# A layer norm with GELU: ten of 64 tiles take their statistics on ScalarE, and beta's split moves

**Chip, cores, metric.** One core of one Trainium2 chip. The metric is the device time of one execution in microseconds (us). Medians and ratios are of fast runs alone, and every profiled run was a fast one, with a granted clock of 1.0. "Span" is the time from the first to the last instruction in a profiled execution; it is some 1.8 us shorter than the device time.

## What is computed

```python
# x: (8, 1024, 2048) float32, gamma, beta: (2048,), eps = 1e-5
mean = np.mean(x, axis=-1, keepdims=True)
var = np.var(x, axis=-1, keepdims=True)
out = gamma * (x - mean) / np.sqrt(var + eps) + beta
return 0.5 * out * (1 + np.tanh(np.sqrt(2 / np.pi) * (out + 0.044715 * out ** 3)))
```

The 8192 rows are 64 tiles of 128 rows by 2048 columns, 1 MB each.

## The kernel before

```python
groups = [2, 2] + [4] * 14 + [2, 1, 1]        # tiles whose 1/sqrt is taken together

def reciprocal_sqrt(nc, pool, ve, n):          # all on GpSimd, on 128 x n
    nc.gpsimd.tensor_scalar(out=y..., in0=ve..., ...)           # first guess from the bits (L23)
    for _ in range(3):                                          # Newton
        nc.gpsimd.tensor_tensor(out=t, in0=y, in1=y, op=MUL)    # L26
        nc.gpsimd.tensor_tensor(out=t, in0=t, in1=ve, op=MUL)   # L27
        nc.gpsimd.tensor_scalar(out=t, in0=t, scalar1=-0.5, scalar2=1.5, op0=MUL, op1=ADD)  # L28
        nc.gpsimd.tensor_tensor(out=y, in0=y, in1=t, op=MUL)    # L29
    return y

def stats(i):                                  # VectorE, then GpSimd once a group
    # [cut: st, mv]
    for c in range(nbank):
        nc.vector.bn_stats(out=st[:, c, :], in_=xts[i][:, c * BANK:(c + 1) * BANK])  # L111
    nc.vector.bn_aggr(out=mvs[g][:, k, :], in_=st)                                   # L112
    if k == size - 1:
        # ve = var + eps (L115); y = reciprocal_sqrt(...); nmr = -(mean * y) (L118, L119)

def normalize(j):                              # ScalarE: y * x + nmr, in place (L125)
def affine(j):                                 # VectorE: ps[j % 2] = xt * gamma (L130),
                                               # TensorE adds beta from b_rows (L133)
def gelu(j):                                   # ScalarE: ps -> xt (L137), store, load tile j + 16

# step s: stats(s); normalize(j); affine(j - 1); gelu(j - 2).
# In the middle j = s - 5: a group's first tile is normalized two steps after
# the statistics of its last.
```

The two tiles `ps` in PSUM, the memory in which TensorE adds beta, matter: a multiplication (`affine(j)`) must wait for `gelu(j - 2)`, which reads the same one. Every engine takes its instructions in program order. [Cut: pools, loads of the first 20 tiles, the launch.]

## Time and profile before

| | before |
|---|---|
| device time, median | 342.36 us |
| span | 340.6 us |
| VectorE busy | 310.5 us (91%) |
| ScalarE busy | 247.6 us (73%) |
| GpSimd busy | 132.3 us (39%) |
| moved by DMA | 135.4 MB, 398 GB/s mean |

In the groups of the profile a row is: line, engine, operation, output and input, count; busy us and mean ns of one; idle time of the engine just ahead of these, and what ended it. In a timeline a row is: start, us, engine, line, operation, count; in brackets the engine's wait ahead of it.

### The profile page before, as it was taken

Reading aid. Unit: us, or ns where it says so; the run is one execution under the profiler, and the core shown is the slowest. Engines: PE = TensorE matmul, PEld = TensorE weight load, DVE = VectorE, ACT = ScalarE, POOL = GpSimd, SP = SyncE. Lnnn points to the kernel's source line nnn. Section 1 sums busy time; section 2 is a strip of 40 time slices with the busy share of each in tenths; the row PEclk is TensorE's granted clock in tenths of the full one; section 3 lists DMA queues with packets and bytes.
Section 4 is the critical chain, followed back from the end, with each engine's and each line's share of the span. In section 5 each row is a group of like instructions: output and inputs, shape, how many; then the busy total and the mean of one; then the engine's idle time right before and its main releaser. Section 6 shows DMA issues by size and latency. Waiting matters only on the chain.

```text
span 340.6 us, 1787 instructions
## 1 busy us (share of the span) xinstructions
PE 122.6 (36%) x264; PEld 35.0 (10%) x264; DVE 310.5 (91%) x391; ACT 247.6 (73%) x130; POOL 132.3 (39%) x308
## 2 busy tenths in 40 slices
PE   4003242343234324432443244324432443245521
PEld 1000010111011101110111011101110111011100
DVE  3799999999999999999999999999999999996640
ACT  0149297886959598786959688695969868698962
POOL 0350307043250806234170714325080523788820
DMA  7999999999999999999999999999999999865556
GB/s 298 416 420 418 420 420 422 428 425 423 425 427 426 426 423 425 425 427 424 427 427 426 425 426 425 427 426 423 426 427 424 426 425 424 352 255 246 247 216 277
DMA packets 19164, 135.41 MB, mean 398 GB/s; under 512 B 2640, under 2 KB 2640, under 8 KB 2640
## 3 DMA queue, kind: packets, MB, share of 16 engines
q1 hardware_dynamic: 18576, 135.27, 94.9%
q10 hardware_dynamic: 576, 0.02, 0.1%
q14 instruction: 10, 0.08, 0.1%
q8 instruction: 2, 0.03, 0.0%
HBM read 68.17 MB, written 67.11 MB: 397 GB/s over the span
## 4 chain that ended last, share of the span: by engine, by line
issue 45%; POOL 36%; DVE 10%; DMA 5%; ACT 1%; PE 1%; POOLq 0%; SPq 0%; ACTq 0%
POOL t L26 12%; POOL ve L115 9%; DVE st L111 6%; POOL t L28 5%; DMA xt<-in_x_dram 4%; DVE ps L130 4%; POOL y L29 4%; POOL t L27 3%; POOL nmr L118 2%; DMA bt<-in_beta_dram 1%; ACT xt L137 1%; POOL nmr L119 1%; POOL y L23 1%; PE ps L133 1%; DVE mv L112 0%
## 5 line engine op out<-in xcount | busy, mean ns | idle before, releaser
L133 PE MATMUL ps<-b_rows,ones 3*128 3x512 bf16 x256 | 119.0, 616 | 209.8 <-DVE ps L130 209.8
L125 ACT ACTIVATE xt<-xt,nmr,y 128x2048 f32<-128x2048 f32 x64 | 133.4, 2086 | 54.8 <-POOL nmr L119 54.8
L111 DVE BATCH_NORM_STATS2 st<-xt 128x6 f32<-128x512 f32 x256 | 157.2, 676 | 2.3 <-DMA xt<-in_x_dram 2.2
L130 DVE TENSOR_TENSOR ps<-xt,g_t 128x2048 f32<-128x2048 f32 x64 | 145.6, 2276 | 10.3 <-ACT xt L137 10.3
L137 ACT ACTIVATE xt<-ps 128x2048 f32<-128x2048 f32 x64 | 119.4, 1868 | 24.0 <-PE ps L133 23.9
L115 POOL TENSOR_SCALAR ve<-mv 128x4 f32<-128x4 f32 (+2 forms) x19 | 31.7, 1666 | 169.6 <-DVE mv L112 169.4
L133 PEld LDWEIGHTS <-ones 3*128 3x128 bf16 x256 | 34.0, 133 | 294.8 <-issue 294.8
L26 POOL TENSOR_TENSOR t<-y 128x4 f32<-128x4 f32 (+2 forms) x57 | 44.6, 782 | 4.6
L112 DVE BATCH_NORM_AGGREGATE mv<-st 128x2 f32<-128x24 f32 x64 | 16.9, 264 | 3.2
L28 POOL TENSOR_SCALAR t<-t 128x4 f32<-128x4 f32 (+2 forms) x57 | 17.3, 303 | 5.0
L29 POOL TENSOR_TENSOR y<-y,t 128x4 f32<-128x4 f32 (+2 forms) x57 | 13.3, 233 | 4.8
L27 POOL TENSOR_TENSOR t<-t,ve 128x4 f32<-128x4 f32 (+2 forms) x57 | 11.4, 199 | 4.5
L125 ACT ACT_TABLE_LOAD x1 | 1.3, 1283 | 9.3 <-DVE st L111 9.3
L118 POOL TENSOR_TENSOR nmr<-mv,y 128x4 f32<-128x4 f32 (+2 forms) x19 | 5.9, 310 | 1.5
L119 POOL TENSOR_SCALAR nmr<-nmr 128x4 f32<-128x4 f32 (+2 forms) x19 | 4.3, 229 | 1.7
L82 DVE CAST part<-bt 128x16 bf16<-128x16 f32 x3 | 0.5, 174 | 4.7 <-DMA bt<-in_beta_dram 4.6
L23 POOL TENSOR_SCALAR y<-ve 128x4 int32<-128x4 int32 (+2 forms) x19 | 3.7, 194 | 1.6
L91 PE MATMUL ps<-zeros 1*128 1x512 bf16 x8 | 3.6, 626 | 1.3 <-DVE zeros L78 1.3
L91 PEld LDWEIGHTS <-zeros 1*128 1x128 bf16 x8 | 1.0, 137 | 3.0 <-issue 1.7
L137 ACT ACT_TABLE_LOAD x1 | 1.3, 1283 | 0.0
L76 DVE MEMSET ones<- 3x128 bf16 x1 | 0.2, 165 | 0.8 <-PEq L191 0.8
L84 DVE TENSOR_TENSOR bt<-bt,part 128x16 f32<-128x16 f32 x2 | 0.3, 175 | 0.1
(5 smaller groups left out, 0.7 us busy)
## 6 DMA issues: line engine op xcount, KB each, us to landing
xt<-in_x_dram SPq DMA_DIRECT2D x64, 1024.0 KB, 19.1
out_dram<-xt SPq DMA_DIRECT2D x64, 1024.0 KB, 17.0
g_t<-in_gamma_dram SPq DMA_DIRECT2D x1, 1024.0 KB, 11.5
b_rows<-part ACTq DMA_DIRECT2D x3, 4.0 KB, 9.9
bt<-in_beta_dram ACTq DMA_DIRECT2D x1, 8.0 KB, 5.1
```

The costliest lines, as they stand in the source:

```text
L26: nc.gpsimd.tensor_tensor(out=t, in0=y, in1=y, op=MUL)
L27: nc.gpsimd.tensor_tensor(out=t, in0=t, in1=ve, op=MUL)
L28: nc.gpsimd.tensor_scalar(out=t, in0=t, scalar1=-0.5, scalar2=1.5, op0=MUL, op1=ADD)
L29: nc.gpsimd.tensor_tensor(out=y, in0=y, in1=t, op=MUL)
L111: nc.vector.bn_stats(out=st[:, c, :], in_=xts[i][:, c * BANK:(c + 1) * BANK])
L112: nc.vector.bn_aggr(out=mvs[g][:, k, :], in_=st)
L115: nc.gpsimd.tensor_scalar(out=ve, in0=mvs[g][:, :, 1], scalar1=float(eps), scalar2=None, op0=ADD)
L118: nc.gpsimd.tensor_tensor(out=nmr, in0=mvs[g][:, :, 0], in1=y, op=MUL)
L125: nc.scalar.activation(out=xts[j], in_=xts[j], func=ACTF.Identity, scale=y[:, k:k + 1], bias=nmr[:, k:k + 1])
L130: nc.vector.tensor_tensor(out=pt, in0=xts[j], in1=g_t, op=MUL)
L133: nc.tensor.matmul(pt[:, s], lhsT=ones, rhs=b_rows[:, s], start=False, stop=True, skip_group_check=True)
L137: nc.scalar.activation(out=xts[j], in_=ps[j % 2], func=ACTF.Gelu_apprx_tanh)
```

## The change

The intent is to take work from VectorE, which had no idle time in the middle, and give it to ScalarE, which had. Ten tiles (8, 12, 16, 24, 28, 32, 40, 44, 48, 56; each the first of its group of four) get their mean from an Identity pass with an accumulator output and their variance from a Square pass, both on ScalarE. Beta's split into three bf16 parts, which waits for beta to arrive, moves behind the second tile's statistics.

```diff
-    for r in range(3):  ...split beta, store the parts to b_rows...
+    def split_beta(): ...the same...
+    on_scalar = {4 * g for g in range(2, 15) if g % 4 != 1}
+    # [cut: junk, a bf16 tile for the passes' unused output; sums, which keeps neg; allocations]
+    def scalar_mean(i):
+        nc.scalar.activation(out=junk, in_=xts[i], func=ACTF.Identity, accum_out=sm)
+        nc.gpsimd.tensor_scalar(out=neg, in0=sm, scalar1=-1.0 / d, ...)
+        nc.gpsimd.tensor_scalar(out=mvs[g][:, k, 0:1], in0=sm, scalar1=1.0 / d, ...)
+        sums[i] = neg
+    def scalar_var(i):
+        nc.scalar.activation(out=junk, in_=xts[i], func=ACTF.Square, bias=sums.pop(i), accum_out=sq)
+        nc.gpsimd.tensor_scalar(out=mvs[g][:, k, 1:2], in0=sq, scalar1=1.0 / d, ...)
     def stats(i):
+        if i in on_scalar:
+            return
     # in step s:
         stats(step)
+        if step == 1: split_beta()
         # [normalize, affine, gelu]
+        if step in on_scalar: scalar_mean(step)
+        if step - 2 in on_scalar: scalar_var(step - 2)
```

In the new kernel the lines are numbered anew: L135 and L136 are the statistics, L154 the multiplication, L149 the normalization, L161 GELU, L115 and L124 the two passes, L139 and L143 the first and last operation of GpSimd's chain.

More of the change, by code (lines that the diff above doesn't have):

```diff
@@ L79, with split_beta @@
     b_rows = singles.tile([3, d], BF16)
-    for r in range(3):
-        part = singles.tile([P, d // P], BF16, name=f"part{r}")
-        nc.vector.tensor_copy(out=part, in_=bt)
-        if r < 2:
-            nc.vector.tensor_tensor(out=bt, in0=bt, in1=part, op=SUB)
-        nc.scalar.dma_start(out=b_rows[r:r + 1, :], in_=part)
+    def split_beta():
+        for r in range(3):
+            part = singles.tile([P, d // P], BF16, name=f"part{r}")
+            nc.vector.tensor_copy(out=part, in_=bt)
+            if r < 2:
+                nc.vector.tensor_tensor(out=bt, in0=bt, in1=part, op=SUB)
+            nc.scalar.dma_start(out=b_rows[r:r + 1, :], in_=part)
     ps = []
@@ L99 @@
     assert sum(groups) == ntiles
+    on_scalar = {4 * g for g in range(2, 15) if g % 4 != 1}
+    junk = singles.tile([P, d], BF16)
     of_tile = []
@@ L103 @@
     mvs, scales = {}, {}
+    sums = {}
+    def scalar_mean(i):
+        g, k, _ = of_tile[i]
+        sm = gsmall.tile([P, 1], F32, name="sm")
+        nc.scalar.activation(out=junk, in_=xts[i], func=ACTF.Identity, accum_out=sm)
+        neg = gsmall.tile([P, 1], F32, name="neg")
+        nc.gpsimd.tensor_scalar(out=neg, in0=sm, scalar1=-1.0 / d, scalar2=None, op0=MUL)
+        nc.gpsimd.tensor_scalar(out=mvs[g][:, k, 0:1], in0=sm, scalar1=1.0 / d, scalar2=None, op0=MUL)
+        sums[i] = neg
+    def scalar_var(i):
+        g, k, _ = of_tile[i]
+        sq = gsmall.tile([P, 1], F32, name="sq")
+        nc.scalar.activation(out=junk, in_=xts[i], func=ACTF.Square, bias=sums.pop(i), accum_out=sq)
+        nc.gpsimd.tensor_scalar(out=mvs[g][:, k, 1:2], in0=sq, scalar1=1.0 / d, scalar2=None, op0=MUL)
     def stats(i):
@@ L149 @@
             stats(step)
+            if step == 1:
+                split_beta()
         take = 1 if step < ntiles else 2
@@ L167 @@
                     break
+        if step in on_scalar:
+            scalar_mean(step)
+        if step - 2 in on_scalar:
+            scalar_var(step - 2)
         ready += pending
```

## The prediction

> **What bounds the kernel now.** I read the page first: busy shares and the slices.
>
> ```profile
> PE 122.6 (36%) x264; PEld 35.0 (10%) x264; DVE 310.5 (91%) x391; ACT 247.6 (73%) x130; POOL 132.3 (39%) x308
> ...
> DVE  3799999999999999999999999999999999996640
> ACT  0149297886959598786959688695969868698962
> ...
> DMA  7999999999999999999999999999999999865556
> ```
>
> Two rows are full at once from slice 3 to slice 34: VectorE (DVE) and the transfers. ScalarE (ACT) has holes. So I looked for the prices (the page's groups) and for who waits (the waits).
>
> ```profile
> L125 ACT ACTIVATE xt<-xt,nmr,y 128x2048 f32<-128x2048 f32 x64 | 133.4, 2086 | 54.8 <-POOL nmr L119 54.8
> L111 DVE BATCH_NORM_STATS2 st<-xt 128x6 f32<-128x512 f32 x256 | 157.2, 676 | 2.3 <-DMA xt<-in_x_dram 2.2
> L130 DVE TENSOR_TENSOR ps<-xt,g_t 128x2048 f32<-128x2048 f32 x64 | 145.6, 2276 | 10.3 <-ACT xt L137 10.3
> L137 ACT ACTIVATE xt<-ps 128x2048 f32<-128x2048 f32 x64 | 119.4, 1868 | 24.0 <-PE ps L133 23.9
> ```
>
> VectorE waits 10.3 us for ScalarE in five places, all in the last 30 us, and 2.2 us for a load at the start. In between it never waits: one tile is statistics (L111, L112) and the multiplication (L130). Then the timeline of one group of four tiles, ScalarE's rows and two of GpSimd's:
>
> ```profile
> 150.63 2.08 ACT L125 ACTIVATE xt<-xt,nmr,y 128x2048 f32<-128x2048 f32 x1
> 153.71 1.88 ACT L137 ACTIVATE xt<-ps 128x2048 f32<-128x2048 f32 x1 [1.00 <-PE ps L133]
> 158.20 2.09 ACT L125 ACTIVATE xt<-xt,nmr,y 128x2048 f32<-128x2048 f32 x1 [2.61 <-POOL nmr L119]
> 160.20 1.86 ACT L137 ACTIVATE xt<-ps 128x2048 f32<-128x2048 f32 x1
> ...
> 170.12 2.08 ACT L125 ACTIVATE xt<-xt,nmr,y 128x2048 f32<-128x2048 f32 x1
> ```
> ```profile
> 149.65 2.18 POOL L115 TENSOR_SCALAR ve<-mv 128x4 f32<-128x4 f32 x1 [10.98 <-DVE mv L112]
> ...
> 154.44 2.29 POOL L26 TENSOR_TENSOR t<-y 128x4 f32<-128x4 f32 x1
> ```
>
> A group lasts 170.12 - 150.63 = 19.49 us, which is VectorE's time. ScalarE works four pairs: starts 158.20 to 160.20 to 161.96 give 2.00 and 1.76, so 3.75 us a pair and 15.0 us a group. Its other 4.5 us are waits: 2.6 for GpSimd's chain, 1.0 and twice 0.56 for TensorE. Two of GpSimd's fifteen small operations take 2.2 us in place of 0.2; both stand exactly beside a multiplication of VectorE (149.49 and 154.41).
>
> Last, the transfer queue late in the kernel:
>
> ```profile
> 245.57 0.34 SPq L63 DMA_DIRECT2D xt<-in_x_dram  x1
> ...
> 250.49 0.34 SPq L63 DMA_DIRECT2D xt<-in_x_dram  x1
> ...
> 255.40 0.34 SPq L63 DMA_DIRECT2D xt<-in_x_dram  x1
> ```
>
> Loads go out every 4.92 us, later than the stores ahead of them would allow, so the queue is full too: a load and a store per tile at 425 to 427 GB/s. But loads run ahead. Load 63 is issued at 265.29 and takes about 19 us (issue to landing), so it is there near 284.5; its statistics start at 302.8. Load 20 (59.61) leads by some 15 us, load 36 (131.7) by some 21 (VectorE's starts counted back from 302.81 at 4.87 a tile). The transfers don't bind until VectorE is about 15 us earlier.
>
> **What the Trainium skill says.** "ScalarE: Activation LUTs", What ACT_TABLE_LOAD costs: 186 ns + 0.833 ns an element, about 93 ns more for each per-partition pointer operand, and neighbours overlap by about 93 ns. For L125 (two pointers, 2048 elements) that is 2078 ns; the trace has 2086. "SBUF — State Buffer", Who interferes with whom: a VectorE instruction with two SBUF inputs contends with a GpSimd instruction that reads SBUF, and the later one waits until the first is done. The trace agrees: the 2.18 and 2.29 us above. "DMA: Bandwidth & Descriptors", Specifications: a fabric ceiling of 435 GB/s and about 358 GB/s of HBM for a core; the trace moves 426, so the first is the one to compare with. No page I read prices the accumulator output.
>
> **The change, part by part.**
> *Removed:* ten statistics on VectorE. From one multiplication's start to the next is 4.87 us with a statistic between, and 2.19 (half of the 4.47 of the pair at 305.55) without: 2.68 us each, 26.8 in all. If VectorE stayed the bound and nothing else bound, that would be 8%.
> *Added on ScalarE:* for each of these tiles an Identity with accumulator (no pointer; estimate from the page 1.89 us, 1.8 to 1.9 after overlap) and a Square (one pointer, the negative mean; 1.99, so 1.9 to 2.0 after overlap). Together 3.8 us, up to 4.1 if the accumulator costs something. The order on the engines shows two table loads in the new kernel as before, so no table is switched.
> *Added on GpSimd:* three 128x1 operations a tile, about 0.3 us each; the last stands ahead of the group's chain.
> *Moved:* beta's split. VectorE waited 4.6 us for beta before its first statistics (6.75). They can now start when tile 0 is in. But the fourth tile's statistics waited for its load until 16.96 anyway, behind 4 MB of earlier transfers, so nearly all of this ends in that wait. I count 0.3 us.
>
> *One changed group.* VectorE needs 19.49 - 2.68 = 16.8 us, ScalarE 15.0 + 3.8 = 18.8, the transfers 4 x 4.92 = 19.7 with a lead in hand. **ScalarE becomes the bound** in a run of changed groups, and the gain is 19.49 - 18.8 = 0.7 us, not 2.68.
>
> *Into a run.* I laid out one group by hand, counting from 150.63. The Identity falls into the 2.6 us hole ahead of the group's first normalization, which is good. But with the statistics gone two multiplications stand back to back (-1.14 to 1.05 to 3.24), and the second holds GpSimd's second operation for another 2.2 us. The chain then meets the next multiplication at 5.93 and is done near 9.1 rather than 7.5. So the first normalization moves from 7.57 to 9.1, the GELU behind it ends at 13.0 rather than 11.4, and the multiplication that needs both (PSUM has two buffers) starts at 13.0; it was 13.49. VectorE was free at 10.8. Of 2.68 us the first group keeps 0.5. The Square delays the next group's start on ScalarE; from there ScalarE is packed, at 18.8 a group.
> Carried on: the second group of a run is 0.8 ahead in all, the third 1.5. The unchanged fourth group is VectorE's again (19.49) and lets ScalarE catch up: at its end ScalarE stands to VectorE as at the start, so nothing further is won or lost.
>
> *Sum.* The runs are tiles 8, 12, 16; 24, 28, 32; 40, 44, 48; and 56 alone. The first run enters worse: step 8 stands at 37.07, right beside GpSimd's first chain of four (37.23), and I count 0.4. The others 1.5 each, tile 56 alone 0.5, start 0.3: 4.2 us. If the accumulator adds a tenth or two to each pass, about 0.5 less. The tail, the last 35 us after the last statistics, is unchanged. 342.4 - 3.9 = **338.5 us**.
>
> **The rivals.**
> *VectorE's gain comes through.* If GpSimd's chain were not held a second time, or the Square cost nothing on the path, the first group would keep about 2 us and each run 3 to 4: 10 to 12 us, near 331. For it: ScalarE is idle 4.5 us a group, and 3.8 fits in that if all holes are usable, which a careful choice of tiles suggests. Against it: only the 2.6 us hole is met by an added pass; the others come from TensorE and vanish only when ScalarE itself is late.
> *The transfers bind.* Then load 63 lands near 284.5 whatever VectorE does, and with sixteen stores left at 2.5 us the span cannot be below some 321 us. It takes over only after 15 us of gain; I don't expect to see it.
> *It gets slower.* The Square and its GpSimd operation now release the group's chain: the Square ends about 0.7 us after the group's last statistics, and the operation behind it may be held by a multiplication. If a second hold falls in every group, a changed group takes about 20 us, and the time is 345. Against it: in the packed state VectorE stands idle about 2 us between multiplications, waiting for GELU, and the chain gets eight operations through there.
>
> **Range and chances.** The sum hangs on small holes, so the error may be as large as the gain: a changed group between 18.5 and 19.4 us gives 335 to 341. I take 334.8 to 342.2. Two per cent is 6.8 us, under 335.5: it needs half of the first rival, 17%. Over 349 there is only the third rival doubled: 2%. Within: 81%.
>
> **What would show it.** Right: VectorE's busy time near 284 us, now with about 20 us of waits on ScalarE's GELU (L137 of before) in the middle of the kernel; ScalarE at about 286 us busy, 85% of the span; changed groups 18.8 to 19 us apart, the fourth 19.5; GpSimd's chain with three long operations where a run starts; the first multiplication hardly earlier than 22.5. Wrong: VectorE still 97% busy in the middle (the gain came through), loads among VectorE's waits (the transfers bind), passes well off 1.9 and 2.0 us, or a ScalarE that still waits 2 us for GpSimd inside a run.

## The result

**339.12 us** (339.01 to 339.14) against 342.36 us: ratio 0.9903, 95% interval 0.9886 to 0.9921. That is 1% faster, inside 2%, and 0.6 us from the predicted 338.5. (A ratio is the mean time of one kernel's fast runs over that of the other's of the same rounds, so not quite the ratio of the medians quoted.)

The page of the new kernel, busy shares and slices:

```profile
PE 122.7 (36%) x264; PEld 34.9 (10%) x264; DVE 285.4 (85%) x341; ACT 283.4 (84%) x170; POOL 149.1 (44%) x338
...
DVE  3899967979999977989999977998999969996640
ACT  0239299999989779999989869999989869998962
...
DMA  8999999999999999999999999999999999976556
```

VectorE lost 25 us of work and now has holes in the middle; ScalarE gained 36 us and has three full stretches (slices 6 to 11, 16 to 20, 25 to 29): these are the three runs of changed groups. The span shrank by 3.3 us only. Where the rest of VectorE's 25 us went is in the waits:

```profile
DVE ps L154 <- ACT xt L161: 33.4, 15, 4.3
ACT xt L149 <- POOL nmr L143: 28.3, 11, 6.8
...
ACT xt L161 <- PE ps L157: 7.7, 9, 2.5
...
DVE st L135 <- DMA xt<-in_x_dram: 5.9, 3, 4.4
```

(Columns: who waited for whom; us in total, times, longest.) VectorE's multiplications waited 10.3 us for GELU, now 33.4. ScalarE's waits for GpSimd fell from 54.8 to 28.3 and those for TensorE from 23.9 to 7.7: the new passes were put into them. Loads cost VectorE nothing in the middle; its three waits for them are all in the first 19 us.

The two passes and what they bring with them, from the groups by shape:

```profile
L124 ACT ACTIVATE junk<-xt,neg 128x2048 bf16<-128x2048 f32 x10 | 20.1, 2007 | 0.0
L115 ACT ACTIVATE junk<-xt 128x2048 bf16<-128x2048 f32 x10 | 19.1, 1911 | 0.0
...
L124 ACT ACTIVATION_READ_ACCUMULATOR junk<-xt,neg 128x1 f32 x10 | 2.1, 207 | 0.0
L115 ACT ACTIVATION_READ_ACCUMULATOR junk<-xt 128x1 f32 x10 | 2.0, 203 | 0.0
```

There is an instruction that the source does not show, which reads the accumulator out. It overlaps with the pass and with what follows.

**Inside a run.** ScalarE's timeline in the second run (tiles 24, 28, 32), the first normalization after each Square:

```profile
129.34 2.09 ACT L149 ACTIVATE xt<-xt,nmr,y 128x2048 f32<-128x2048 f32 x1
...
148.19 2.10 ACT L149 ACTIVATE xt<-xt,nmr,y 128x2048 f32<-128x2048 f32 x1
...
167.03 2.12 ACT L149 ACTIVATE xt<-xt,nmr,y 128x2048 f32<-128x2048 f32 x1
```

148.19 - 129.34 = 18.85 and 167.03 - 148.19 = 18.84 us a group, with ScalarE never idle in between; before it was 19.49. The two passes with their read-outs add 18.85 - 15.0 = 3.85 us.

**Into a run.** GpSimd's chain and ScalarE at the start of the same run (tile 24). VectorE's line comes first: two multiplications in one row, because the statistics between them are gone.

```profile
109.22 4.47 DVE L154 TENSOR_TENSOR ps<-xt,g_t 128x2048 f32<-128x2048 f32 x2
...
123.75 2.30 DVE L154 TENSOR_TENSOR ps<-xt,g_t 128x2048 f32<-128x2048 f32 x1 [2.46 <-ACT xt L161]
```
```profile
109.38 2.18 POOL L139 TENSOR_SCALAR ve<-mv 128x4 f32<-128x4 f32 x1 [10.69 <-DVE mv L136]
111.64 2.09 POOL L23 TENSOR_SCALAR y<-ve 128x4 int32<-128x4 int32 x1
113.81 0.20 POOL L26 TENSOR_TENSOR t<-y 128x4 f32<-128x4 f32 x1
...
116.34 2.32 POOL L27 TENSOR_TENSOR t<-t,ve 128x4 f32<-128x4 f32 x1
```
```profile
110.36 2.08 ACT L149 ACTIVATE xt<-xt,nmr,y 128x2048 f32<-128x2048 f32 x1
...
115.22 1.90 ACT L115 ACTIVATE junk<-xt 128x2048 bf16<-128x2048 f32 x1
...
119.86 2.09 ACT L149 ACTIVATE xt<-xt,nmr,y 128x2048 f32<-128x2048 f32 x1 [2.65 <-POOL nmr L143]
```

Three of GpSimd's sixteen operations are held now, not two ("held": over 2 us in place of 0.2, beside a multiplication of VectorE): 109.38 and 111.64 beside the two multiplications of the pair, and 116.34 beside the next one. The first normalization of the group starts 119.86 - 110.36 = 9.50 us after the last of the group before; in the kernel before it was 158.20 - 150.63 = 7.57. VectorE then waits 2.46 us for the GELU behind it, which is nearly the 2.68 us that the missing statistics had saved.

**Sum over the kernel**, by the start of certain tiles' statistics on VectorE:

| statistics of tile | before | after | ahead | gained since the row above |
|---|---|---|---|---|
| 5 | 24.68 | 23.75 | 0.93 | 0.93 (start) |
| 23 | 107.83 | 106.55 | 1.28 | 0.35 (first run) |
| 39 | 185.79 | 183.57 | 2.22 | 0.94 (second run) |
| 55 | 263.76 | 260.59 | 3.17 | 0.95 (third run) |
| 63 | 302.81 | 299.56 | 3.25 | 0.08 (tile 56 alone) |

After the last statistics the kernels take 37.8 and 37.7 us.

Within the second run the three groups gain 0.08, 0.24 and 0.63 us (the statistics of tiles 23, 27, 31 and 35 start 1.28, 1.36, 1.60 and 2.23 us ahead). So the entry costs the gain of the first group and most of that of the second; only from the third on does a group gain the full 19.49 - 18.85 = 0.64. The first run enters differently: there the missing statistics stood beside other statistics, so no two multiplications meet, and one operation of the chain is held (38.87, 2.21 us) where none was before; its first group loses 0.52 us.

### The profile page after: what moved, and what is told of

Its sections match the earlier page's. It is cut to its first block, busy times and chain, and to the rows that moved or that the text cites. A ratio compares the mean times of both kernels' runs of the same rounds, so it can differ in the third digit from the quotient of the medians.

```text
span 337.3 us, 1799 instructions
## 1 busy us (share of the span) xinstructions
PE 122.7 (36%) x264; PEld 34.9 (10%) x264; DVE 285.4 (85%) x341; ACT 283.4 (84%) x170; POOL 149.1 (44%) x338
## 4 chain that ended last, share of the span: by engine, by line
DMA 30%; DVE 28%; POOL 16%; ACT 13%; issue 9%; PE 1%; ACTq 0%; SPq 0%; POOLq 0%; DVEq 0%
DMA xt<-in_x_dram 16%; DVE st L135 14%; DVE ps L154 13%; DMA out_dram<-xt 10%; ACT xt L161 7%; ACT xt L149 5%; DMA b_rows<-part 4%; POOL t L28 3%; POOL t L27 2%; POOL t L26 2%; POOL y L29 2%; POOL ve L139 2%; DVE mv L136 1%; POOL y L23 1%; ACT junk L124 1%
## 5 line engine op out<-in xcount | busy, mean ns | idle before, releaser
L154 DVE TENSOR_TENSOR ps<-xt,g_t 128x2048 f32<-128x2048 f32 x64 | 145.6, 2280 | 33.4 <-ACT xt L161 33.4
L149 ACT ACTIVATE xt<-xt,nmr,y 128x2048 f32<-128x2048 f32 x64 | 134.0, 2094 | 28.3 <-POOL nmr L143 28.3
L135 DVE BATCH_NORM_STATS2 st<-xt 128x6 f32<-128x512 f32 x216 | 132.8, 677 | 5.9 <-DMA xt<-in_x_dram 5.9
L161 ACT ACTIVATE xt<-ps 128x2048 f32<-128x2048 f32 x64 | 119.7, 1872 | 7.7 <-PE ps L157 7.7
L125 POOL TENSOR_SCALAR mv<-sq 128x1 f32<-128x1 f32 x10 | 16.7, 1672 | 83.5 <-ACT junk L124 83.5
L139 POOL TENSOR_SCALAR ve<-mv 128x4 f32<-128x4 f32 (+2 forms) x19 | 12.2, 643 | 58.9 <-DVE mv L136 47.3
L27 POOL TENSOR_TENSOR t<-t,ve 128x4 f32<-128x4 f32 (+2 forms) x57 | 25.6, 449 | 4.5
L29 POOL TENSOR_TENSOR y<-y,t 128x4 f32<-128x4 f32 (+2 forms) x57 | 23.6, 414 | 4.8
L28 POOL TENSOR_SCALAR t<-t 128x4 f32<-128x4 f32 (+2 forms) x57 | 23.4, 411 | 5.0
L124 ACT ACTIVATE junk<-xt,neg 128x2048 bf16<-128x2048 f32 x10 | 20.1, 2007 | 0.0
L115 ACT ACTIVATE junk<-xt 128x2048 bf16<-128x2048 f32 x10 | 19.1, 1911 | 0.0
L26 POOL TENSOR_TENSOR t<-y 128x4 f32<-128x4 f32 (+2 forms) x57 | 15.5, 271 | 4.6
L136 DVE BATCH_NORM_AGGREGATE mv<-st 128x2 f32<-128x24 f32 x54 | 14.2, 263 | 2.9
L117 POOL TENSOR_SCALAR neg<-sm 128x1 f32<-128x1 f32 x10 | 10.6, 1055 | 7.1 <-ACT junk L115 7.1
L143 POOL TENSOR_SCALAR nmr<-nmr 128x4 f32<-128x4 f32 (+2 forms) x19 | 4.4, 233 | 1.7
## 6 DMA issues: line engine op xcount, KB each, us to landing
b_rows<-part ACTq DMA_DIRECT2D x3, 4.0 KB, 10.3
```

The costliest lines, as they stand in the source:

```text
L115: nc.scalar.activation(out=junk, in_=xts[i], func=ACTF.Identity, accum_out=sm)
L124: nc.scalar.activation(out=junk, in_=xts[i], func=ACTF.Square, bias=sums.pop(i), accum_out=sq)
L139: nc.gpsimd.tensor_scalar(out=ve, in0=mvs[g][:, :, 1], scalar1=float(eps), scalar2=None, op0=ADD)
L149: nc.scalar.activation(out=xts[j], in_=xts[j], func=ACTF.Identity, scale=y[:, k:k + 1], bias=nmr[:, k:k + 1])
L154: nc.vector.tensor_tensor(out=pt, in0=xts[j], in1=g_t, op=MUL)
L161: nc.scalar.activation(out=xts[j], in_=ps[j % 2], func=ACTF.Gelu_apprx_tanh)
```

## The experiments

The theory after the result: *inside a run of changed groups ScalarE is the bound at 18.85 us a group and each group from the third on gains 0.64 us; each entry to a run (its first two groups) gains almost nothing, because GpSimd's chain, held once more, takes VectorE's 2.68 us back; beta's move is worth 0.9 us.* The rivals: each tile gives the same small share; ScalarE's passes alone are what takes the gain; the transfers bind.

| kernel | median us | ratio to before | 95% interval |
|---|---|---|---|
| changed kernel | 339.12 | 0.9903 | 0.9886, 0.9921 |
| beta_only | 341.32 | 0.9963 | 0.9951, 0.9976 |
| scalar_only | 340.09 | 0.9931 | 0.9919, 0.9944 |
| seven_in_a_row | 338.60 | 0.9884 | 0.9869, 0.9899 |
| seven_apart | 341.41 | 0.9965 | 0.9953, 0.9978 |
| no_passes | 341.85 | 0.9985 | 0.9971, 0.9998 |
| one_step | 327.26 | 0.9560 | 0.9547, 0.9573 |
| before_one_step | 339.56 | 0.9919 | 0.9906, 0.9933 |
| no_passes_one_step | 327.83 | 0.9575 | 0.9562, 0.9589 |
| newton2 | 331.72 | 0.9686 | 0.9672, 0.9699 |
| thirteen_in_a_row | 334.60 | 0.9769 | 0.9755, 0.9782 |
| thirteen_newton2 | 330.59 | 0.9652 | 0.9639, 0.9666 |

The kernel before measured 342.37 to 342.51.

### 1 and 2. Each part alone

```diff
 # beta_only
-    on_scalar = {4 * g for g in range(2, 15) if g % 4 != 1}
+    on_scalar = set()
 # scalar_only: split_beta() called where the split stood before
```

> No tile's statistics on ScalarE; only beta's split is moved. Theory (the move is worth the 0.93 us by which the changed kernel's sixth statistics start earlier, 23.75 against 24.68): 341.4 us. Rival A (the start is lost in the wait for the fourth tile, as I had predicted, 0.3 us): 342.1. Rival B (the move is the whole gain): 339.1.

> Ten tiles on ScalarE, beta's split where it was. Theory (runs worth 0.4 + 0.9 + 0.9 + 0.1): 340.0 us. If the two parts are not additive, say because the first run depends on the start, it is off by over 0.3. Rival B: 342.4.

Measured 341.32 and 340.09. The medians lie 1.17 and 2.40 us under 342.49, together 3.57; the changed kernel lies 3.24 under. So the parts add up to within 0.33 us, less than the intervals of the ratios leave open, and neither is the whole. Rivals A and B fall.

Why beta's move is worth three to four times what I had predicted is at the start of the queue's timeline, before and after:

```profile
5.83 31.69 SPq L63 DMA_DIRECT2D xt<-in_x_dram  x17
```
```profile
2.79 10.64 SPq L63 DMA_DIRECT2D xt<-in_x_dram  x5
```

The load of tile 3 used to wait for beta's transfer (the queue's waits of before have 3.0 us for it); now it is issued 3.0 us earlier (in beta_only as well, at 2.89). And on VectorE, before and after, the statistics of tiles 3 and 4:

```profile
16.96 2.47 DVE L111 BATCH_NORM_STATS2 st<-xt 128x6 f32<-128x512 f32 x4 [2.20 <-DMA xt<-in_x_dram]
19.81 2.48 DVE L111 BATCH_NORM_STATS2 st<-xt 128x6 f32<-128x512 f32 x4
```
```profile
15.69 2.47 DVE L135 BATCH_NORM_STATS2 st<-xt 128x6 f32<-128x512 f32 x4 [1.12 <-DMA xt<-in_x_dram]
18.88 2.48 DVE L135 BATCH_NORM_STATS2 st<-xt 128x6 f32<-128x512 f32 x4 [0.42 <-DMA xt<-in_x_dram]
```

VectorE still waits for tile 3, as predicted, but tile 3 lands 1.27 us sooner (beta_only: 1.35), and then tile 4 is waited for. Whether it lands sooner because it was issued sooner, or because beta's rows are no longer sent out in small packets beside it, no run separates. The traces speak for the first: in the first 15.6 us the queues moved 352 GB/s before and 357 in beta_only, a difference of 0.08 MB, which by estimate is 0.2 us at 425 GB/s; but the load of tile 4 was issued 0.5 us after that of tile 3 before, and 3.1 us after it in the changed kernel.

### 3 and 4. The same work, in a row and apart

```diff
-    on_scalar = {4 * g for g in range(2, 15) if g % 4 != 1}
 # seven_in_a_row
+    on_scalar = {4 * g for g in range(2, 9)}
 # seven_apart
+    on_scalar = {4 * g for g in range(2, 15, 2)}
```

> Tiles 8, 12, ..., 32: seven in one run, beta moved. Theory (only groups inside a run gain, 19.49 - 18.85 = 0.64 us each; the entry gains about nothing): start 0.93 + first run of three 0.43 + 4 x 0.64 = 3.9 us, so 338.5. Rival (each tile gives the same, (3.25 - 0.93) / 10 = 0.23 us): 339.8, the same as the seven apart.

> Tiles 8, 16, ..., 56: seven, each alone between two unchanged groups; busy times of every engine as in seven_in_a_row. Theory (each is an entry, whose gain GpSimd's chain takes back: 2.68 us of VectorE's work go, and 0.1 us is kept): start 0.93, first one -0.5, six of 0.1: 341.4 us. Rival (each tile gives the same 0.23 us): 339.8.

Measured 338.60 and 341.41. The busy times are the same (VectorE 292.9 and 293.0 us, ScalarE 272.5 and 273.1), and the arrangement alone makes 2.8 us. The seven apart are worth nothing at all over the move of beta (341.32): in the trace the first loses 0.5 us and each of the others gains 0.08. The seven in a row give more than the change's ten with gaps. The rival of equal shares is out.

### 5. ScalarE's passes taken away

```diff
 def scalar_mean(i):
-    ...Identity pass, neg, mv...
+    nc.gpsimd.memset(mvs[g][:, k, 0:1], 0.0)
+    nc.gpsimd.memset(mvs[g][:, k, 1:2], 1.0)
 def scalar_var(i):
-    ...Square pass, mv...
+    return
```

> Wrong on purpose: the ten tiles' mean and variance are the constants 0 and 1 (written by GpSimd memsets), no pass on ScalarE. Theory (GpSimd's chain, held three times by VectorE's multiplications because two stand back to back, sets a changed group's time when ScalarE's passes do not): a group 19.5 us, as before, and about 341 us, so SLOWER than the changed kernel although it does 39 us less on ScalarE. Rival A (ScalarE's passes are the bound): groups of VectorE's 16.8 us, the time falls to the transfers' floor, 323 to 328.

Measured 341.85, that is 2.7 us *slower* than the changed kernel, with 38 us less of ScalarE work (245.4 against 283.4 us busy). It passed the comparison in spite of its constants, as the input's rows have means near 0 and variances near 1, so passing says little about accuracy. The second group of the same run, on ScalarE and on GpSimd:

```profile
120.66 2.09 ACT L143 ACTIVATE xt<-xt,nmr,y 128x2048 f32<-128x2048 f32 x1 [4.54 <-POOL nmr L137]
...
140.21 2.09 ACT L143 ACTIVATE xt<-xt,nmr,y 128x2048 f32<-128x2048 f32 x1 [4.46 <-POOL nmr L137]
```
```profile
129.67 2.10 POOL L133 TENSOR_SCALAR ve<-mv 128x4 f32<-128x4 f32 x1 [8.98 <-DVE mv L130]
131.86 0.19 POOL L23 TENSOR_SCALAR y<-ve 128x4 int32<-128x4 int32 x1
132.13 2.25 POOL L26 TENSOR_TENSOR t<-y 128x4 f32<-128x4 f32 x1
...
136.99 2.32 POOL L28 TENSOR_SCALAR t<-t 128x4 f32<-128x4 f32 x1
```

A group takes 140.21 - 120.66 = 19.55 us with three operations held, though VectorE has 16.8 us of work and ScalarE 15.0. Without the passes VectorE's multiplications come earlier and fall on the chain again. So two bounds lie close together: ScalarE at 18.85, and the chain at 19.5 where nothing delays VectorE. Taking either one away alone should show the other; the passes alone have now been taken.

### 6, 7, 8. The chain cut short

```diff
-    for _ in range(3):
+    for _ in range(1):
 # one_step: in the changed kernel; before_one_step: in the kernel before; no_passes_one_step: in no_passes
```

> The changed kernel with one Newton step in place of three (8 operations in the chain in place of 16; less exact, an estimated error of 2e-3 at most). Theory: the chain ends near 5.1 us after the group's start, inside ScalarE's Identity pass, so the entry of each run is no longer held: 2.5 us more in each of the four entries, and up to 3 us in the tail, where the last normalization waits for the chain: 326 to 330 us. Rival (only ScalarE's passes bind): the tail's gain alone, as in before_one_step, 336 to 338.

> Control: the kernel before with one Newton step. In the middle VectorE is the bound without waits, so nothing is gained there; in the tail the last normalization waits 2.7 us for the chain. Both theories: 339.5 to 341 us.

> Both suspected costs taken away (wrong on purpose as no_passes, and one Newton step). Theory: changed groups at VectorE's 16.8 us until the loads' lead of 15 to 20 us is used up, then the transfers bind: VectorE waits for loads near the end, 322 to 328 us. If neither the passes nor the chain were the bound, it stays above 335.

Measured 327.26, 339.56 and 327.83. In the kernel before, the short chain is worth 2.8 us, all of it in the tail (its last statistics start at 303.06, not earlier than 302.81). In the changed kernel it is worth 11.9. At the entry of the second run ScalarE is no longer held:

```profile
110.66 1.90 ACT L115 ACTIVATE junk<-xt 128x2048 bf16<-128x2048 f32 x1
112.46 0.19 ACT L115 ACTIVATION_READ_ACCUMULATOR junk<-xt 128x1 f32 x1
112.55 2.08 ACT L149 ACTIVATE xt<-xt,nmr,y 128x2048 f32<-128x2048 f32 x1
```

The normalization follows the Identity pass at once, 112.55 - 105.81 = 6.74 us after the last one of the group before (9.50 in the changed kernel). The chain itself ends 5.08 us after that start rather than 9.46: of the 4.38 us, eight operations make 8 x 0.28 = 2.24, and 2.1 is the third hold, which no longer falls in it; the two beside the pair are still there. Inside a run a group still takes ScalarE's time: 140.87 - 122.03 = 18.84 us. No run takes the hold away and keeps the chain's length, so the two are separated in the timeline alone.

The last statistics start at 286.90, which is 12.7 us earlier than in the changed kernel: 4.6 us by the end of the first run, 2.8 in the second and third, 2.6 at tile 56. Of these 12.7 us and the tail's 2.8 only 11.9 reach the end. The last GELU ends at 316.9 and the span at 325.4: 8.5 us for the last stores, where the kernel before takes 5.0 and the changed one 4.9. There the transfers bind: the queues move 426 to 429 GB/s in slices 34 to 39, where they had fallen to 216 to 255 in slices 36 to 39 of the kernel before.

With both costs gone (no_passes_one_step) VectorE does wait for loads in the middle:

```profile
215.39 2.47 DVE L129 BATCH_NORM_STATS2 st<-xt 128x6 f32<-128x512 f32 x4 [2.81 <-DMA xt<-in_x_dram]
...
255.20 2.47 DVE L129 BATCH_NORM_STATS2 st<-xt 128x6 f32<-128x512 f32 x4 [2.81 <-DMA xt<-in_x_dram]
```

and ends no earlier than one_step. So the transfers' floor for this order of work seems to be near 327 us: two kernels that differ by 35 us of ScalarE work both end there. One Newton step leaves a relative error of 1.8e-3 in 1/sqrt (worked out on the host over the range 0.25 to 4, with the same start), so this is an experiment and no version to keep.

### 9, 10, 11. Versions that keep the accuracy

```diff
 # newton2
-    for _ in range(3):
+    for _ in range(2):
 # thirteen_in_a_row
-    on_scalar = {4 * g for g in range(2, 15) if g % 4 != 1}
+    on_scalar = {4 * g for g in range(2, 15)}
 # thirteen_newton2: both
```

> The changed kernel with two Newton steps in place of three (12 operations in the chain; an estimated relative error of 5e-6). Theory: at the entry of a run the first two operations are still held, nine go free, and only the last of the twelve is held by the third multiplication, so the chain ends near 8.3 us after the group's start instead of 9.5: some 1.1 us for each of four entries, and 1 to 2 us in the tail: 332.5 to 334.5 us. Rival (a chain counts only through its operations, 4 x 0.28 us, or not at all): 336.5 to 338.

> Tiles 8, 12, ..., 56 without the three gaps: one entry, thirteen groups at ScalarE's 18.85 us. Theory: start 0.93 + first run of three 0.43 + 10 x 0.64 = 7.8 us: 334.6. Rival (the gaps are needed because ScalarE falls ever further behind, or the transfers bind): no better than the ten tiles' 339.1.

> Both: thirteen tiles in one run, and two Newton steps. Theory: 7.8 us as thirteen_in_a_row, one entry of 1.1, the tail's 1 to 2: 331 to 333 us, still above the transfers' floor of about 326. If the two overlap because both shorten the same wait, 334.

Measured 331.72, 334.60 and 330.59. Thirteen in a row came out to the tenth: 0.64 us for each further group, and the gaps that the change leaves cost it 4.5 us. Two Newton steps gave 7.4 us, 0.8 more than the expected range: the last statistics start 4.5 us earlier (295.07 against 299.56), 1.1 for each of four entries as expected, and the tail gives 2.8 instead of 1 to 2. The entry of the second run shows the twelfth and last operation held, and no more:

```profile
115.22 2.36 POOL L143 TENSOR_SCALAR nmr<-nmr 128x4 f32<-128x4 f32 x1
```

The two together gain less than their sum (4.5 + 7.4 = 11.9; measured 8.5), as expected: one run has one entry to relieve. The time is 0.4 us below the expected range, because the tail gave 2.8 us here too. thirteen_newton2, 330.59 us, is the best that keeps the result (relative error of 1/sqrt 4.7e-6, worked out in the same way): 3.5% faster than the kernel before.

## Why the prediction was right, by its own steps

- *ScalarE becomes the bound in a run, at 18.8 us.* Right: 18.85. The passes' spacing of 3.8 us was 3.85; the accumulator's read-out costs 0.2 us each but only about 0.1 of the path (61.70 - 59.80 = 1.90 from an Identity to the next normalization, where the prediction had 1.8 to 1.9).
- *The hole of 2.6 us takes the Identity, and GpSimd, held once more, takes the gain back.* Right in mechanism: the chain is what no_passes (still slow without passes) and one_step (fast with them) show, and the added hold stands in the timeline. The size was off: the chain ended at 9.5, not 9.1 us. The trace has four short operations of 0.28 us behind the third hold, and 9.1 leaves room for about three; the prediction counts fifteen operations, where the timeline of before has sixteen. The first group of a run therefore keeps 0.1 us, not 0.5: tile 56 alone gave 0.08, and the seven apart gave nothing.
- *A run of three gains 1.5.* Too high: 0.95. The prediction has 0.5, 0.8 and 1.5 after each of its groups, the trace 0.08, 0.32 and 0.95: the first is short by the 0.4 just named, and the steps behind it were right to 0.1. The first run's 0.4 was 0.35.
- *The unchanged fourth group starts afresh.* Right: the second and third run gain the same, 0.94 and 0.95.
- *Beta's move, 0.3 us.* The step that failed: "nearly all of this ends in that wait", with the first multiplication hardly earlier than 22.5; it starts at 21.57. The wait itself moved, since the fourth tile's load no longer stood behind beta's transfer. It is worth 0.93 us in the trace and 1.17 in the medians, about a third of the whole gain.
- *The tail is unchanged; the transfers do not bind.* Right: 37.8 and 37.7 us, and no load is waited for after 19 us. They seem to bind at a span of 325.4 us (one_step), above the prediction's floor of some 321. Its own terms, 284.5 and sixteen stores at 2.5 us, add up to 324.5.
- *A reading that was off without effect:* "twice 0.56" among ScalarE's waits. The group has it once; 2.61 + 1.00 + 0.56 = 4.2 us, and the other 0.3 of the 4.5 comes from the three instructions that have nothing right behind them to overlap with (2.08 us in place of a spacing of 1.99 for a normalization).
- *The busy times and waits:* VectorE 285.4 us (284 predicted), ScalarE 283.4 (286), VectorE's added waits for GELU 23.1 (about 20).
- The two errors of size, 0.6 too little for beta and 1.6 too much for the runs and tile 56, partly cancel, and 0.3 had been taken off for the accumulator. That the sum was closer than its terms is luck.

## What to carry to other kernels

Work moved off a full engine is worth only what the next bound leaves, and that bound can be a chain of small operations that a third engine holds up: here removing an instruction pushed two multiplications together, and the pair held GpSimd. Before counting such a gain, lay out one period by hand with the timeline's starts; it gave each group here to half a microsecond. Where changed periods have a cost of entry, put them in one run, and shorten the chain that sets the entry.

## What the Trainium skill lacked or had wrong

- "ScalarE: Activation LUTs", What ACT_TABLE_LOAD costs: no price for the accumulator output. Here each pass with one brings a separate ACTIVATION_READ_ACCUMULATOR of 203 to 207 ns, of which about 0.1 us lies on the path. Its formula held for the passes: 1.89 and 1.99 us worked out, 1.91 and 2.01 measured.
- "SBUF — State Buffer", Who interferes with whom: the lock is described for one instruction against one. With two multiplications back to back on VectorE, GpSimd gets one operation done between the two and is held again: 2.18 us and 2.09 us for operations of 0.2, at the entries of the second and third run and of tile 56.
- "DMA: Bandwidth & Descriptors", Specifications: the row of the HBM limit, about 358 GB/s for a core, carries no condition, and this one core exceeds it throughout, with 415 to 429 GB/s of loads and stores in slices 2 to 35 of the changed kernel; only the fabric figure of 435 compares. Further down, under "Measured", the same page gives the figure for both cores of an HBM domain streaming at once, so it is this condition that the row lacks.
